# GpSimd adds the kept outer sum to C22 in SBUF and narrows each group's last row tile, with the orders of groups, beginning and end replaced

## The chip, the core and the metric

One core of one Trainium2 chip runs the kernel. TensorE (PE) multiplies matrices into PSUM, which has eight banks of 128 x 512 fp32 numbers, called b0 to b7 below. VectorE (DVE), ScalarE (ACT) and GpSimd (POOL) work on tiles of 128 partitions. SyncE (SP) issues all data transfers of this kernel, in one queue. Each engine works through its own instructions in order and waits on semaphores for the others. The metric is the time of one execution in microseconds (us).

## The reference

```python
def reference(x, w):
    cs = np.cumsum(x, axis=1)
    diff = cs - np.concatenate([np.zeros(...), cs[:, :-1, :]], axis=1)
    return np.matmul(diff, w).astype(np.float32)
```

The difference of a running sum is `x` again, so the kernel computes `x @ w`: x is 8 x 2048 x 2048, which is 16384 rows in 128 row tiles of 128, and w is 2048 x 2048, all fp32.

## The kernel before

**Beginning.** While `w` is loaded, the first four row tiles are multiplied in bf16 in the plain way (lines 347 and 394). VectorE and ScalarE then make scaled fp16 blocks of `w` (B11, B12, B21, B22 and the differences T1 to T4), and a first group of four row tiles is done by `group_plain`.

**Groups.** The other 120 row tiles are done in 30 groups of four, `group(g)`, in which the row tiles g and h = g + 2 give the upper halves A11, A12 and g + 1 and h + 1 the lower halves A21, A22. The outer scheme is Strassen's in Winograd's form with seven products: five of them, called P1 to P5, are split once more into seven inner products (`Quarters`), and S2 T2 and S3 T3 are done directly. One inner product, `slot(i)`, is four 128x512 matmuls (line 624); a piece of a direct product is four too (line 602). All banks are in use all the time. In `Quarters`, bank h[0] gathers one inner product after another; ScalarE copies it away in between: `first` copies the first product into g[0], on which slot 3 then accumulates, and `out2` and `out4` copy h[0] into SBUF, after which slots 4 and 6 write h[0] again. `middle` and `last` (line 590) are VectorE's sums of a bank and such a copy. `s1` to `s4`, the sums S1 to S4 and the sums `in1` to `in5` of weights are VectorE's sums of two fp16 operands in SBUF, line 590 too.

**Ends of the outer sums.** Bank pair X holds, late in a group, a sum that both C22 and C21 need. ScalarE keeps it, scaled, in SBUF as the beginning of C21 (`keep`, line 145), and VectorE adds it, scaled, to C22 out of the bank (`add_one`, line 649: bank times a factor plus C22). The same is done for Y, of the tiles h. When a result is whole, SP puts it to HBM (line 657, 669 for the last group).

**The next group's rows.** Each row tile is loaded in two halves (`load`, line 159), weighed by ScalarE (`weigh`, line 167: a sum of absolute values; `mean`, line 188), given a scale by VectorE (`scale`, a reciprocal, line 190), narrowed to fp16 with that scale by ScalarE (`narrow`, two halves of 128x1024, line 145) and turned by two DMA transposes (`turn`, line 218). Labels carry the tile's role: 4 and 6 are the next group's g and h, 5 and 7 its g + 1 and h + 1. So `narrow7.0` and `narrow7.1` narrow the last row tile of the next group. They run early in that group; S1h is the first sum that reads the tile, P5.s1 reads S1h, and the second product of P5 reads P5.s1.

**What sets the order.** The code only records operations, each with a label and an engine. A table of numbers, `places`, gives each label a place for the periods 0 (beginning), 1, 2, 29, 30, 31 and one common row (`None`) for all other groups; `emit` sorts all operations by it, and the engines' queues stand in that order.

Of the kernel before, what the change touches and what calls it, by code (L numbers as in the profile page):

```python
# [10 lines left out]
def kernel(  # L11
# [6 lines left out]
    nc = tc.nc  # L18
# [130 lines left out]
    def role(t):  # L149
        return t - PLAIN - 4 * period[0]  # L150
# [49 lines left out]
    def narrow_one(t, i):  # L200
        to, data, s = narrowed(t)[:, ds(i * NH, NH)], where[t][i], scales[t]
        record(f"narrow{role(t)}.{i}", "act", on_two(to, data, s))
        if i == 1 and t != PLAIN + 1:
            stage.append(where[t][1])
# [442 lines left out]
    def add_one(label, c, p, u):  # L647
        record(
            label, "dve", lambda: nc.vector.scalar_tensor_tensor(c, p, u, c, MUL, ADD)  # L649
        )  # L650

# [312 lines left out]
    def group(g):  # L964
# [206 lines left out]
        add("C22g+X", C22g, X, vg, [1])  # L1171
        keep("keep C21g", X, vg, C21g, [1])
        add("C22g+X", C22g, X, vg, [0])
# [23 lines left out]
        add("C22h+Y", C22h, Y, vh, [0])  # L1197
        keep("keep C21h", Y, vh, C21h, [1])
        add("C22h+Y", C22h, Y, vh, [1])
# [21 lines left out]
    for g in range(PLAIN + 4, END, 4):  # L1221
# [201 lines left out]
        },  # L1423
# [211 lines left out]
```

## Time and profile before

| what | before |
|---|---|
| median of 3 runs | 1448.48 us (1448.45 to 1448.72) |
| span of the profiled execution | 1446.9 us |
| granted TensorE clock | 0.999 |
| PE, DVE, ACT, POOL busy | 1439.8, 1339.8, 1193.8, 0.9 us |
| bytes moved by DMA | 351.59 MB, mean 243 GB/s |

The span is one execution as the hardware profiler saw it; the runs are timed from outside. Rows of groups read: line, engine, operation, output from input, shapes, count, busy time and mean duration of one, then the idle time of the engine just before and what ended it. Matmuls are pipelined: each has a duration of 379 ns, while the next one starts 0.216 us after it. Times on the time line and of the stretches are microseconds from the beginning of the span.

### The profile page before, as it was taken

How to read it: one execution, taken by the hardware profiler on the slowest of the kernel's cores; microseconds unless marked ns; L12 is line 12 of the kernel's file. 1: busy time of each engine (PE TensorE's matmuls, PEld its weight loads, DVE VectorE, ACT ScalarE, POOL GpSimd, SP SyncE). 2: the span in 40 equal slices, each digit the busy share in tenths (PEclk: the TensorE clock that was granted, in tenths of full speed). 3: DMA queues.
4: the chain of work that ended last, by engine and by line, in shares of the span. 5: the costliest groups of instructions: out<-in, count | busy, mean ns of one | idle time of the engine just before them, and what ended most of it. 6: DMA issues, size and time to landing. Idle time of an engine off the chain costs nothing.

```text
span 1446.9 us, 20369 instructions
## 1 busy us (share of the span) xinstructions
PE 1439.8 (100%) x6698; PEld 652.8 (45%) x6698; DVE 1339.8 (93%) x2355; ACT 1193.8 (83%) x1985; POOL 0.9 (0%) x5
## 2 busy tenths in 40 slices
PE   9999999999999999999999999999999999999998
PEld 4444444444444444444444444444444444444443
DVE  7999999999999999999999999999999999999988
ACT  4897878898888888888988888988888888889783
POOL 0000000000000000000000000000000000000000
PEclk9999999999999999999999999999999999999999
DMA  9999988899888999988898989998989998899963
GB/s 362 375 266 265 250 227 222 230 249 264 231 229 223 243 256 241 242 227 229 245 263 219 245 220 242 245 264 217 236 231 242 265 236 237 216 235 249 275 190 116
DMA packets 343930, 351.59 MB, mean 243 GB/s; under 512 B 270992, under 2 KB 270992, under 8 KB 343824
## 3 DMA queue, kind: packets, MB, share of 16 engines
q1 hardware_dynamic: 343824, 350.29, 89.4%
q8 instruction: 52, 0.85, 0.2%
q14 instruction: 54, 0.44, 0.1%
HBM read 150.99 MB, written 134.22 MB: 197 GB/s over the span
## 4 chain that ended last, share of the span: by engine, by line
PE 93%; issue 4%; DVE 1%; ACT 1%; DMA 0%; POOLq 0%; DVEq 0%
PE b L624 61%; PE b L602 32%; DVE W L146 1%; DMA out_dram<-arena 0%; ACT arena L145 0%; DVE arena L649 0%; ACT waste L167 0%; ACT F L145 0%; ACT arena L141 0%; PE b L490 0%; POOLq L1630 0%; DVE b L590 0%; DVEq L1630 0%; ACT b L141 0%; ACT tiny L194 0%
## 5 line engine op out<-in xcount | busy, mean ns | idle before, releaser
L602 PE MATMUL b<-W,x 128*128 128x512 f16 x2144 | 518.3, 379 | 0.0
L649 DVE SCALAR_TENSOR_TENSOR arena<-b,tiny,arena 128x512 f32<-128x512 f32 x612 | 448.0, 747 | 15.0 <-ACT arena L141 4.5
L624 PEld LDWEIGHTS <-arena 128*128 128x128 f16 x2744 | 268.3, 98 | 324.5 <-DVE arena L590 5.4
L624 PE MATMUL b<-W,arena 128*128 128x512 f16 x1672 | 413.8, 379 | 0.0
L145 ACT ACTIVATE arena<-b,tiny 128x512 f32<-128x512 f32 x495 | 316.3, 684 | 31.9 <-PE b L602 13.7
L602 PEld LDWEIGHTS <-x 128*128 128x128 f16 x2144 | 209.7, 98 | 253.1 <-DVE x L590 0.2
L167 ACT ACTIVATE waste<-F,tiny 128x1024 uint8<-128x1024 f32 x246 | 284.0, 1154 | 16.2 <-DMA F<-in_x_dram 14.7
L145 ACT ACTIVATE F<-F,tiny 128x1024 f16<-128x1024 f32 x245 | 280.9, 1147 | 11.7 <-DVE tiny L190 10.6
L624 PE MATMUL b<-W,x 128*128 128x512 f16 x1192 | 288.1, 379 | 0.0
L624 PE MATMUL b<-arena 128*128 128x512 f16 x1072 | 261.6, 379 | 0.1
L624 PEld LDWEIGHTS <-x 128*128 128x128 f16 x1428 | 139.7, 98 | 168.5
L590 DVE TENSOR_TENSOR b<-b,arena 128x512 f32<-128x512 f32 x298 | 206.4, 693 | 5.4 <-ACT arena L141 1.9
L141 ACT COPY arena<-b 128x512 f32<-128x512 f32 (+1 forms) x316 | 181.6, 586 | 27.1 <-PE b L624 16.2
L141 ACT COPY b<-b 128x512 f32<-128x512 f32 x149 | 85.6, 574 | 136.6 <-PE b L624 113.3
L590 DVE TENSOR_TENSOR arena<-W 128x2048 f16<-128x2048 f16 (+1 forms) x158 | 186.0, 1177 | 0.2 <-PE b L624 0.2
L590 DVE TENSOR_TENSOR arena<-x,x 128x512 f16<-128x512 f16 (+1 forms) x181 | 91.9, 508 | 50.5 <-PE b L624 50.4
L590 DVE TENSOR_TENSOR x<-x,x 128x1024 f16<-128x1024 f16 x124 | 85.4, 689 | 1.9
L590 DVE TENSOR_TENSOR arena<-W,arena 128x512 f16<-128x512 f16 (+1 forms) x157 | 86.3, 566 | 0.2 <-PE b L624 0.2
L590 DVE TENSOR_TENSOR arena<-arena 128x512 f16<-128x512 f16 x120 | 50.9, 425 | 13.7 <-PE b L624 11.8
L624 PE MATMUL b<-arena,x 128*128 128x512 f16 x236 | 60.4, 379 | 0.0
L347 PE MATMUL b<-arena 128*128 128x512 bf16 x240 | 53.8, 379 | 0.6 <-DVE arena L142 0.4
L590 DVE TENSOR_TENSOR arena<-x,arena 128x512 f16<-128x512 f16 x119 | 49.9, 419 | 0.3 <-PE b L624 0.3
(51 smaller groups left out, 494.8 us busy)
## 6 DMA issues: line engine op xcount, KB each, us to landing
F<-in_x_dram SPq DMA_DIRECT2D x246, 512.0 KB, 5.5
out_dram<-arena SPq DMA_DIRECT2D x240, 512.0 KB, 4.8
W<-in_w_dram SPq DMA_DIRECT2D x31, 512.0 KB, 9.0
out_dram<-arena SPq DMA_DIRECT2D x31, 256.0 KB, 2.7
W<-in_x_dram SPq DMA_DIRECT2D x16, 256.0 KB, 7.2
x<-F SPq DMA_TRANSPOSE x246, 4.3
arena<-in_x_dram SPq DMA_DIRECT2D x2, 512.0 KB, 5.0
W<-in_w_dram SPq DMA_DIRECT2D x2, 256.0 KB, 9.3
```

Of the source, the lines that this page charges most:

```text
L141: "act": lambda: nc.scalar.copy(to, src),
L145: "act": lambda: nc.scalar.activation(to, src, COPY, scale=scale),
L146: "dve": lambda: nc.vector.tensor_scalar(to, src, scale, None, MUL),
L167: lambda: nc.scalar.activation(waste, data, ABS, bias=least, scale=1.0 / ROW, accum_out=m),
L347: said = nc.tensor.matmul(to[n], xP[:, r, ko, :], b[:, ds(n * NB, NB)], start=(ko == 0), stop=(ko == KO - 1),)
L590: record(label, "dve", lambda: nc.vector.tensor_tensor(dst, p, q, op))
L602: said = nc.tensor.matmul(to[n], a[k], b[k][:, n, :], start=(start and k == 0), stop=(k == KH - 1), skip_group_check=True,)
L624: said = nc.tensor.matmul(to, a[k], b[k], start=(start and k == 0), stop=(k == 3), skip_group_check=True)
L649: label, "dve", lambda: nc.vector.scalar_tensor_tensor(c, p, u, c, MUL, ADD)
```

## The change

Three things change. First, the four adds of X and Y to C22 in each group of the loop read the kept copy in SBUF, not the bank, and are done by GpSimd (`sum_kept`). Second, in every period but the first, GpSimd narrows the row tile of role 7. Third, the rows 1, 2, 29, 30, 31 and `None` of `places` are replaced; row 0 stays as it was.

```diff
     def narrow_one(t, i):
         to, data, s = narrowed(t)[:, ds(i * NH, NH)], where[t][i], scales[t]
-        record(f"narrow{role(t)}.{i}", "act", on_two(to, data, s))
+        if role(t) == 7 and period[0]:
+            record(
+                f"narrow{role(t)}.{i}",
+                "pool",
+                lambda: nc.gpsimd.tensor_scalar(to, data, s, None, MUL),
+            )
+        else:
+            record(f"narrow{role(t)}.{i}", "act", on_two(to, data, s))
...
+    def sum_kept(label, c, k, halves=range(2)):
+        for n in halves:
+            sum_kept_one(f"{label}.{n}", c[:, n, :], k[:, n, :])
+
+    def sum_kept_one(label, c, k):
+        record(label, "pool", lambda: nc.gpsimd.tensor_tensor(c, c, k, ADD))
...
-        add("C22g+X", C22g, X, vg, [1])
+        sum_kept("C22g+X", C22g, C21g, [0])
         keep("keep C21g", X, vg, C21g, [1])
-        add("C22g+X", C22g, X, vg, [0])
+        sum_kept("C22g+X", C22g, C21g, [1])
...
-        add("C22h+Y", C22h, Y, vh, [0])
+        sum_kept("C22h+Y", C22h, C21h, [0])
         keep("keep C21h", Y, vh, C21h, [1])
-        add("C22h+Y", C22h, Y, vh, [1])
+        sum_kept("C22h+Y", C22h, C21h, [1])
...
         None: {
-            'C21h+P4.h.0': 937, 'P1.0': 943, 'P2.0': 977, 'P1.1': 981, 'P1.first': 1012,
+            'P4.last': 782.515, 'P1.0': 943, 'C21h+P4.h.0': 971.428, 'P1.1': 974.765,
```

The numbers tell little by themselves; what the queues hold does. Three places follow, in which line numbers after the change are 7 to 14 higher.

**PE in the second group of the loop**, at P2's first product (into b6, with x01 as weights). P2's slot 3, into b4 with the same x01, accumulates on ScalarE's copy of b6. After the change:

```order
L631 MATMUL b6_80<-W_58,x01_63 128x512
L631 LDWEIGHTS x01_63
L631 MATMUL b6_80<-W_58,x01_63 128x512
L631 LDWEIGHTS x01_63
L631 MATMUL b6_80<-W_58,x01_63 128x512
L631 LDWEIGHTS x01_63
L631 MATMUL b4_78<-W_58,x01_63 128x512
L631 LDWEIGHTS x01_63
```

Before:

```order
L624 MATMUL b6_80<-W_58,x01_63 128x512
L624 LDWEIGHTS x01_63
L624 MATMUL b6_80<-W_58,x01_63 128x512
L624 LDWEIGHTS x01_63
L624 MATMUL b6_80<-W_58,x01_63 128x512
L624 LDWEIGHTS arena_70
L624 MATMUL b0_74<-arena_70 128x512
L624 LDWEIGHTS arena_70
```

Before, four times five other matmuls stood between the last one into b6 and the first one into b4; now none does.

**VectorE in a group of the common row**, just after the group's first products, around the reciprocal that `narrow7` needs. After the change:

```order
L597 TENSOR_TENSOR arena<-W,arena 128x512 x2
L597 TENSOR_TENSOR arena<-x_66,x_67 128x1024
L597 TENSOR_TENSOR arena<-W,arena 128x512
L597 TENSOR_TENSOR x_66<-x_62,x_66 128x1024
L597 TENSOR_TENSOR arena<-x_62,x_64 128x512
L656 SCALAR_TENSOR_TENSOR arena<-b_79,tiny,arena 128x512
L597 TENSOR_TENSOR arena<-W,arena 128x512
L597 TENSOR_TENSOR arena<-x_62,arena 128x512
L597 TENSOR_TENSOR arena<-x_63,x_65 128x512
L190 RECIPROCAL tiny<-tiny 128x1
```

Before:

```order
L590 TENSOR_TENSOR arena<-W,arena 128x512 x2
L190 RECIPROCAL tiny<-tiny 128x1
L590 TENSOR_TENSOR arena<-x_62,x_64 128x512
L590 TENSOR_TENSOR arena<-W,arena 128x512
L590 TENSOR_TENSOR b_75<-b_77,arena 128x512
L590 TENSOR_TENSOR arena<-W,arena 128x512
L590 TENSOR_TENSOR arena<-x_66,x_67 128x1024
```

The rows from W are the four parts of the weight sum in1.Q4, the rows 128x1024 are S1g and S3g. Before, the reciprocal stood behind two parts of in1.Q4; now it stands behind all four, S1g, S3g, three of the inner sums and a bank's add.

**SP late in a group of the common row**, from the first half of the load of role 7 on (`F<-in_x_dram` is a load, `out_dram<-arena` a put). After the change:

```order
L159 DMA F<-in_x_dram 128x1024
L225 DMA_TRANSPOSE x_67<-F 128x8x128
L225 DMA_TRANSPOSE x_66<-F 128x8x128
L671 DMA out_dram<-arena 128x1024
L159 DMA F<-in_x_dram 128x1024
L671 DMA out_dram<-arena 128x1024
```

Before:

```order
L159 DMA F<-in_x_dram 128x1024
L218 DMA_TRANSPOSE x_66<-F 128x8x128
L159 DMA F<-in_x_dram 128x1024
L218 DMA_TRANSPOSE x_67<-F 128x8x128
L657 DMA out_dram<-arena 128x1024 x2
```

The second half of that load, `load7.1`, stood ahead of both puts of the tile g + 1; now it stands behind the first of them, put1.1, which puts the C22 that GpSimd has added to.

More of the change, by code (lines that the diff above doesn't have):

```diff
@@ L1370 @@
         1: {
[52 rows of a table removed]
-        },
[48 rows of a table removed]
[64 rows of a table added]
+        },
[56 rows of a table added]
         },
         29: {
[43 rows of a table removed]
[52 rows of a table added]
         },
         30: {
[34 rows of a table removed]
[41 rows of a table added]
         },
         31: {
-            'P4.last': 457, 'C21h+P4.h.1': 459, 'put-1.0.1': 469, 'C21h+P4.h.0': 594,
-            'put-1.0.0': 1067,
+            'P4.last': 457.284, 'C21h+P4.h.1': 457.287, 'put-1.0.1': 457.291,
+            'C21h+P4.h.0': 461.468, 'put-1.0.0': 464.683,
         },
         None: {
[43 rows of a table removed]
[53 rows of a table added]
         },
```

482 rows, old and new, of the table places are left out of this document.

## The prediction, made before the changed kernel ran

> **What bounds the kernel now.** I read the head of the page first, then the chain and the waits, then stretches of the span, and single places on the time line last.
>
> ```profile
> span 1446.9 us, 20369 instructions
> PE 1439.8 (100%) x6698; PEld 652.8 (45%) x6698; DVE 1339.8 (93%) x2355; ACT 1193.8 (83%) x1985; POOL 0.9 (0%) x5
> ```
>
> TensorE is busy throughout and GpSimd is empty. A busy PE need not run at its own pace, so I look at the chain that ended last and at everything PE and its weight loads waited for (total, times, longest):
>
> ```profile
> 251.78 12.09 PE b L624 x56
> 295.81 12.09 PE b L624 x56
> ```
>
> ```profile
> PE b L380 <- DVE arena L260: 1.2, 1, 1.2
> PE b L347 <- DVE arena L142: 0.4, 1, 0.4
> PE b L347 <- ACT arena L141: 0.2, 1, 0.2
> PEld L624 <- DVE arena L590: 5.4, 27, 0.3
> ```
>
> The same piece of the chain comes back after 44.03 us, and 12.09 us for 56 matmuls is 0.2159 us each. A group issues 51 runs of four matmuls (a quarter, below: 0.863 us); 204 x 0.2158 = 44.03. So a group is nothing but matmuls at their own pace. The three waits of PE belong to the warm-up and the plain first rows. The fourth row is a warning: about once in a group a weight load waits for a VectorE sum, and the matmul in flight just hides it.
>
> Stretches of the span (after the length: busy time of PE, PEld, DVE, ACT, POOL; then clock, DMA share, GB/s):
>
> ```profile
> 100.00:140.00 40.00, 40.00 (x187) 18.13 (x186) 39.86 (x94) 29.45 (x49) 0.00 (x0) 1.00 0.94 264
> 140.00:180.00 40.00, 40.00 (x187) 18.12 (x186) 39.86 (x78) 33.76 (x58) 0.00 (x0) 1.00 0.95 255
> 600.00:644.03 44.03, 44.03 (x206) 19.95 (x205) 40.77 (x74) 37.48 (x64) 0.00 (x0) 1.00 0.90 239
> 1400.00:1420.00 20.00, 20.00 (x95) 9.05 (x93) 18.97 (x36) 12.16 (x22) 0.00 (x0) 1.00 0.54 165
> ```
>
> PE has no gap in any of them, at clock 1.00. VectorE has 3.3 us to spare in a steady group (44.03 - 40.77), nothing from 100 to 180 us, and 5% near the end. Hence **taking work off VectorE and ScalarE shortens nothing by itself**: no matmul goes away, and PE waits for neither. A gain can only lie behind the last matmul; a loss can arise wherever a result comes later than before.
>
> **The change part by part.** In each of 30 groups four VectorE adds go, in 29 of them two ScalarE narrowings; 120 adds and 58 narrowings come on GpSimd. The rows of the work that goes:
>
> ```profile
> L649 DVE SCALAR_TENSOR_TENSOR arena<-b,tiny,arena 128x512 f32<-128x512 f32 x612 | 448.0, 747 | 15.0 <-ACT arena L141 4.5
> L145 ACT ACTIVATE F<-F,tiny 128x1024 f16<-128x1024 f32 x245 | 280.9, 1147 | 11.7 <-DVE tiny L190 10.6
> 1440.65 2.73 DVE L649 SCALAR_TENSOR_TENSOR arena<-b,tiny,arena 128x512 f32<-128x512 f32 x4
> ```
>
> (a) *Freed time.* Four adds in a row take 2.7 us of VectorE, two narrowings 2.3 us of ScalarE. PE covers both, so they are worth **0**; VectorE's room in a steady group grows from 3.3 to 6.0 us.
>
> (b) *Price on GpSimd.* No row shows such work there. I bound it by the engine that did it (0.75 and 1.15 us) and by twice that (1.5 and 2.3), and take the middle, 1.1 and 1.7: 4 x 1.1 + 2 x 1.7 = 7.8 us a group, between 5.3 and 10.6. The Trainium skill, GPSIMD Engine Reference, section "3.1 Elementwise — side-by-side cycle accounting", gives 4497 ns for a two-input fp32 add of 2048 elements, by which I estimate 1.1 us for 512; its section "4.1 Engine selection" puts one-input work at roughly line rate. If narrowing went as fast as that add (1.1), the start term in (d) would be 1.5 and the whole sum 0.8 us smaller; no run here shows it yet.
>
> (c) *A new order of products.* The first place in the section on the change shows PE going straight from P2's first product in b6 to the product that accumulates on its copy in b4. What that copy takes stands on the time line of before, at the same product:
>
> ```profile
> 165.24 1.03 PE L624 MATMUL b<-W,x 128*128 128x512 f16 x4
> 166.10 1.03 PE L624 MATMUL b<-arena 128*128 128x512 f16 x4
> 166.35 0.57 ACT L141 COPY b<-b 128x512 f32<-128x512 f32 x1
> ```
>
> The copy ends at 166.92, so b4's product could start at about 166.97, where now another starts at 166.10: **0.9** lost, which nothing hides. In the same way I counted, in the built order, the places where a bank is copied by ScalarE and written again with a single quarter between: nine in the last two groups (before: none), and two in each of 26 steady groups (before: none). From the start of the last matmul one quarter gives 0.22 + 0.86 = 1.08 us; the matmul's 0.38, the copy's 0.57 and two hand-overs of some 0.05 need 1.05. In hand are 0.03 us, and a longer ScalarE row in the way (1.15) would cost up to 1.1. I take 0.1 us a place for nine at the end and three at the start, **1.2** (0 to 2.4), and 0.1 for each steady group, **2.6** (from 0).
>
> (d) *GpSimd beside VectorE.* Line 590 holds VectorE's sums; all but those into banks read two operands from SBUF:
>
> ```profile
> 140.00:180.00 40.00, 28.34 (x55) 1.00 0.95 255
> 600.00:644.03 44.03, 27.72 (x50) 1.00 0.90 239
> L590 DVE TENSOR_TENSOR b<-b,arena 128x512 f32<-128x512 f32 x298 | 206.4, 693 | 5.4 <-ACT arena L141 1.9
> ```
>
> Less ten bank rows (6.9 us), two-operand rows fill 20.8 of 44.03 us, 47%; from 140 to 180 us, less some four, 64%. Whether they and GpSimd hold each other up no row here shows. If not, it costs 0. If each us of GpSimd stops VectorE, it costs 10.6 - 2.7 = 7.9 us once, in the loop's first group, where VectorE has no room. I take the share of two-operand rows: 0.64 x 7.8 - 2.7 = **2.3**, and **1.0** (0 to 4) for the last two groups, whose room is a third of a steady one's. In a steady group 0.47 x 7.8 = 3.7 us fit into the 6.0 of room. The rule that speaks most against the change is the Trainium skill's, SBUF — State Buffer, section "Who interferes with whom": a VectorE instruction with two SBUF inputs and a GpSimd instruction that reads SBUF exclude each other for the whole instruction. It is the third rival.
>
> (e) *New waits, and the path of the narrowed tile.* VectorE's add of P4 to C21 must now wait until GpSimd has read C21; behind it stand P2.s1, P2.s2 and the next group's sums, for which P2's and P1's products wait. The put of C22 waits for GpSimd, and behind it, by the third place shown, stands load7.1. That load begins the tightest path: load, weigh, mean, reciprocal, narrow, transpose, S1h, P5.s1, second product of P5.
>
> ```profile
> 741.35 2.33 ACT L145 ACTIVATE F<-F,tiny 128x1024 f16<-128x1024 f32 x2
> 751.43 0.67 DVE L590 TENSOR_TENSOR arena<-x,x 128x1024 f16<-128x1024 f16 x1
> 752.35 2.75 PE L624 MATMUL b<-W,arena 128*128 128x512 f16 x12
> 1436.99 0.42 DVE L590 TENSOR_TENSOR arena<-x,x 128x512 f16<-128x512 f16 x1
> 1437.33 0.69 DVE L590 TENSOR_TENSOR b<-b,arena 128x512 f32<-128x512 f32 x1
> DMA to landing us min/median/max: 3.0/4.3/7.4
> ```
>
> Before, narrowing ends at 743.7 and P5's second product starts at 752.35 + 8 x 0.216 = 754.1: 10.4 us for transposes and sums. After, with the group's first matmul at 0: the weight sum in1.Q4 waits for P1's second product, done at 0.86 + 1.03 = 1.9. By the second place shown, it and the rows up to the reciprocal follow: seven of 128x512 (0.34 from start to start), two of 128x1024 (0.6) and one add (0.7), 4.3 us in all, so narrowing starts near 6.4. In the new order P5's second product is the twentieth quarter, at 19 x 0.863 = 16.4. S1h, P5.s1 and the weight load take 0.7 + 0.4 + 0.2. There remain 8.7 us for two narrowings and a transpose's landing: 2 x 1.7 + 4.3 = 7.7 fits with 1.0 in hand, 2 x 1.15 + 3.0 with 3.4, and 2 x 2.3 + 7.4 is 3.3 late. I take **0**.
>
> **Sum**: 0.9 + 1.2 + 2.6 + 2.3 + 1.0 = 8.0 us on the span of 1446.9, 1454.9. The shown runs' median, 1448.5, lies 1.6 above that span, so **1456.5**; with each term at half or at one and a half, 1452.5 to 1460.5.
>
> **Rivals.** *Not slower* (0.20): GpSimd takes 0.75 and 1.15 us and disturbs nobody, and only the 0.9 of (c) is lost: 1449.4. For it speak 6.0 us of room; against it margins of 0.03.
>
> *Late in every group* (0.20): the wait for the narrowed tile takes the place of VectorE's load. It decides from a narrowing of 2.2 us with a landing of 4.3; at 2.3 us it is 0.2 late, with a landing of 5.1 then 1.0. Between them 0.6 x 28 groups = 17 us on top of the sum: 1473.
>
> *Full exclusion* (0.16): every us of GpSimd stops VectorE where there is no room, 7.9 at the start and 4 at the end in place of 2.3 and 1.0: 1465. It is what the page SBUF — State Buffer of the Trainium skill would make of (d).
>
> *Faster* (0.02): only the tail could give it.
>
> ```profile
> 1440.83 1.03 PE L624 MATMUL b<-W,x 128*128 128x512 f16 x4
> out_dram<-arena SPq DMA_DIRECT2D x31, 256.0 KB, 2.7
> ```
>
> Behind the last matmul's end at 1441.9 lie 5.0 us of which an add (0.7) and a put's landing (2.7) must stay; 1.6 us at most can go, less than 0.2% (2.9 us, about what a measurement of this kernel tells from no change).
>
> **Chances.** The forecast has 0.42. Slower by over 0.2%: 0.42 + 0.20 + 0.16 = 0.78; within: 0.20; faster: 0.02. The range, 1448.6 to 1482, leaves out the best part of the first rival and the worst of the second.
>
> **What would show it.** (a) is right if VectorE is busy some 38 us in a group. (c) is right if PE waits 0.9 us once near 165 us behind a ScalarE copy, and 0.05 to 0.3 at some other copies. (d) is right if two-operand rows start late or grow while GpSimd works, most of all from 150 to 200 us. (e) is wrong if P5's weights come late in every group. The whole is wrong if groups still repeat at 44.03 us from the first to the last (first rival), or at 44.4 and more (second).

## The result, and the profile after

| what | before | after |
|---|---|---|
| median | 1448.47 us (1448.22 to 1448.72) | 1480.13 us (1478.03 to 1481.12) |
| span of the profiled execution | 1446.9 us | 1477.2 us |
| VectorE, ScalarE, GpSimd busy | 1339.8, 1193.8, 0.9 us | 1289.2, 1134.4, 348.3 us |

The changed kernel is slower: the ratio is 1.0217, with a 95% interval of 1.0202 to 1.0231. The direction was forecast, the size was not: 31.7 us were lost in place of 8. One of the four runs of narrow_load10, an experiment below, took 2563.27 us at a granted clock of 0.556; its time below is the median of the other three.

The page of the changed kernel first: its head, then two groups of costly instructions (busy time and mean of one in ns, then the idle time ahead of them):

```profile
span 1477.2 us, 20562 instructions
PE 1450.1 (98%) x6692; PEld 650.9 (44%) x6698; DVE 1289.2 (87%) x2235; ACT 1134.4 (77%) x1927; POOL 348.3 (24%) x183
...
L664 POOL TENSOR_TENSOR arena<-arena 128x512 f32<-128x512 f32 x120 | 179.0, 1508 | 940.9 <-DMA out_dram<-arena 628.3
...
L206 POOL TENSOR_SCALAR F<-F,tiny 128x1024 f16<-128x1024 f32 x58 | 168.4, 2904 | 123.0 <-DVE tiny L190 120.3
```

GpSimd is 348 us busy, where 7.8 us a group had been reckoned, some 234 in all. A narrowing takes 2.9 us, 2.5 times ScalarE's 1.15. What PE itself waited for, against three short waits of the warm-up before:

```profile
PE b L631 <- ACT arena L141: 7.3, 16, 1.0
PE b L631 <- DVE arena L597: 5.2, 11, 1.4
PE b L631 <- ACT arena L145: 2.3, 2, 2.0
PE b L631 <- ACT b L141: 1.9, 3, 0.8
```

ScalarE's copies into SBUF (line 141 into arena: the `out2` and `out4`) and VectorE's sums of weights are late. These idle times are short of the loss: a matmul lasts 0.38 us, but the next one is due 0.22 us after its start, so the first 0.16 us of a late start do not show as idle time. So below, a wait is counted from the start of one matmul to the start of the next, less 0.216, each put down to its inner product. Counted so, the changed kernel loses 3.2 us in the periods 1 and 2, 19.6 in the 26 groups of the common row and 6.6 in the last two; the kernel before 0.5 in all. Behind the last matmul lie 6.1 us in place of 5.0. That makes 30.0 of the 30.3 us between the spans.

Of the 19.6 us, 13.9 stand at one place, **P1.4, the slot 4 of P1, which waits in 25 groups**; 2.8 stand at P5.1, the place that the prediction had watched. Two steady stretches (length, busy time of PE, PEld, DVE, ACT, POOL, then clock):

```profile
600.00:644.60 44.60, 44.25 (x206) 19.87 (x204) 38.97 (x70) 34.88 (x62) 11.79 (x6) 1.00 0.89 235
644.60:689.30 44.70, 44.17 (x206) 19.91 (x205) 38.98 (x68) 35.71 (x63) 11.79 (x6) 1.00 0.89 234
```

A group takes some 44.7 us for the same 44.03 us of matmuls, at clock 1.00. VectorE is only 39 us busy: freeing it was real, and worth nothing.

How P1.4 comes to wait is read backwards on the time line, here in one group: first the instructions of GpSimd's line (shortest, median and longest, ns), then the time line of VectorE, SyncE's queue, ScalarE and PE.

```profile
L664 POOL TENSOR_TENSOR arena<-arena x3: 1267/1268/2317, 520.1 to 523.7; 128x512 f32<-128x512 f32 x3
```

```profile
521.44 1.22 DVE L597 TENSOR_TENSOR arena<-W,arena 128x2048 f16<-128x2048 f16 x1
...
523.81 0.34 SPq L671 DMA_DIRECT2D out_dram<-arena  x1
524.19 0.42 SPq L159 DMA_DIRECT2D F<-in_x_dram  x1
...
529.86 1.15 ACT L167 ACTIVATE waste<-F,tiny 128x1024 uint8<-128x1024 f32 x1 [1.31 <-DMA F<-in_x_dram]
...
531.34 0.56 ACT L141 COPY arena<-b 128x512 f32<-128x512 f32 x1
...
531.96 1.02 PE L631 MATMUL b<-W,arena 128*128 128x512 f16 x4 [0.56 <-ACT arena L141]
```

The second of the three adds, C22g+X.1, is the long one: 2.3 us, because VectorE sums four parts of a weight (in1.Q1, 1.22 us) at the same time. `put1.1` waits for this add; `load7.1`, which the change placed behind that put, goes at 524.19 and has landed only at 529.86. ScalarE has nothing to do but stands in `weigh7.1` for 1.31 us; the copy P1.out2 is queued behind it, and PE waits for the copy.

Two of the forecast losses are there too: P2.3 behind ScalarE's copy of P2's first product, and VectorE's last adds behind GpSimd's last one.

```profile
171.99 1.02 PE L631 MATMUL b<-W,x 128*128 128x512 f16 x4 [0.76 <-ACT b L141]
...
1470.45 1.27 POOL L664 TENSOR_TENSOR arena<-arena 128x512 f32<-128x512 f32 x1 [2.90 <-ACT arena L145]
...
1471.75 1.41 DVE L656 SCALAR_TENSOR_TENSOR arena<-b,tiny,arena 128x512 f32<-128x512 f32 x2 [0.38 <-POOL arena L664]
```

The first is 0.92 us from start to start, against 0.9 forecast. The second belongs to the 1.0 us more behind the last matmul: part (e) of the prediction names such a wait, but gives it no time. In adds_half, below, where GpSimd adds half the columns, 0.2 us of it is left.

### The profile page after: what moved, and what is told of

It is laid out like the page before. It is cut to its first block, busy times and chain, and to the rows that moved or that the text cites. A ratio compares the mean times of both kernels' runs of the same rounds, so it can differ in the third digit from the quotient of the medians.

```text
span 1477.2 us, 20562 instructions
## 1 busy us (share of the span) xinstructions
PE 1450.1 (98%) x6692; PEld 650.9 (44%) x6698; DVE 1289.2 (87%) x2235; ACT 1134.4 (77%) x1927; POOL 348.3 (24%) x183
## 5 line engine op out<-in xcount | busy, mean ns | idle before, releaser
L609 PE MATMUL b<-W,x 128*128 128x512 f16 x2144 | 515.6, 379 | 0.0
L145 ACT ACTIVATE arena<-b,tiny 128x512 f32<-128x512 f32 x495 | 330.5, 685 | 132.5 <-PE b L609 98.9
L656 DVE SCALAR_TENSOR_TENSOR arena<-b,tiny,arena 128x512 f32<-128x512 f32 x492 | 356.1, 745 | 78.6 <-POOL arena L664 31.1
L664 POOL TENSOR_TENSOR arena<-arena 128x512 f32<-128x512 f32 x120 | 179.0, 1508 | 940.9 <-DMA out_dram<-arena 628.3
L631 PE MATMUL b<-W,x 128*128 128x512 f16 x1192 | 301.0, 379 | 2.9 <-ACT arena L145 2.0
L631 PE MATMUL b<-arena 128*128 128x512 f16 x1072 | 267.1, 380 | 1.6 <-ACT b L141 1.2
L145 ACT ACTIVATE F<-F,tiny 128x1024 f16<-128x1024 f32 x187 | 214.7, 1148 | 24.3 <-DVE tiny L190 23.2
L206 POOL TENSOR_SCALAR F<-F,tiny 128x1024 f16<-128x1024 f32 x58 | 168.4, 2904 | 123.0 <-DVE tiny L190 120.3
L597 DVE TENSOR_TENSOR arena<-W,arena 128x512 f16<-128x512 f16 (+1 forms) x157 | 104.8, 683 | 0.0
L597 DVE TENSOR_TENSOR arena<-arena,x 128x512 f16<-128x512 f16 x119 | 50.7, 426 | 4.8 <-DVE arena L597 0.5
```

The source lines that it names most:

```text
L145: "act": lambda: nc.scalar.activation(to, src, COPY, scale=scale),
L206: lambda: nc.gpsimd.tensor_scalar(to, data, s, None, MUL),
L597: record(label, "dve", lambda: nc.vector.tensor_tensor(dst, p, q, op))
L609: said = nc.tensor.matmul(to[n], a[k], b[k][:, n, :], start=(start and k == 0), stop=(k == KH - 1), skip_group_check=True,)
L631: said = nc.tensor.matmul(to, a[k], b[k], start=(start and k == 0), stop=(k == 3), skip_group_check=True)
L664: record(label, "pool", lambda: nc.gpsimd.tensor_tensor(c, c, k, ADD))
```

## The experiments

All times stand beside runs of the kernel before on the same chip, 1448.4 to 1448.7 us. First four kernels that undo or do one part.

**load71_early.** In the common row, `load7.1` goes back ahead of the transposes of role 5:

```diff
-            'load7.1': 2488.37
+            'load7.1': 2360.0
```

> One number of the changed kernel is altered: in the row of the common groups load7.1 goes ahead of both transposes of role 5 and of put1.1 in SyncE's queue. Theory 'queue' (load7.1 lands late because of its new place; ScalarE stands in weigh7.1 until it has landed, and the copy P1.out2, for which TensorE's P1.4 waits, stands behind it): the wait at P1.4, 0.56 us in each of 25 groups, goes, and most of the 2.1 us at P5.1 too, so 1480.1 - 13.9 to - 16 = 1464 to 1467. Theory 'GpSimd' (its rows are too slow, 1.27 and 2.85 us, and whatever comes earlier ahead of them is lost behind them): the wait moves from P1.4 to P5.1, about 0.6 us a group, so 1476 to 1481.

Measured: 1474.95 us (ratio 1.0181, 1.0166 to 1.0196). Neither theory had it whole. Not one wait at P1.4 is left in the common row, as "queue" said, but 11.6 us now stand at P5.1, in all 26 groups, as "GpSimd" said:

```profile
PE b L631 <- DVE arena L597: 8.9, 28, 1.0
```

How P5.1 comes to wait stands on the time line of one group: GpSimd's two narrowings, SyncE's two transposes (the second one is issued at 538.40, when the narrowings end), VectorE's S1h, and PE.

```profile
532.50 5.87 POOL L206 TENSOR_SCALAR F<-F,tiny 128x1024 f16<-128x1024 f32 x2 [4.33 <-DVE tiny L190]
...
535.46 4.17 SPq L225 DMA_TRANSPOSE x<-F  x2
...
541.54 0.69 DVE L597 TENSOR_TENSOR arena<-x,x 128x1024 f16<-128x1024 f16 x1 [1.00 <-DMA x<-F]
...
542.75 1.47 PE L631 MATMUL b<-W,arena 128*128 128x512 f16 x6 [0.25 <-DVE arena L597]
```

VectorE stands 1.00 us for the transposed tile, P5.s1 follows on S1h, and PE waits for P5.s1. So two paths of nearly equal lateness lay beside each other; mending one uncovered the other.

**adds_half.** GpSimd adds half the columns:

```diff
-        record(label, "pool", lambda: nc.gpsimd.tensor_tensor(c, c, k, ADD))
+        record(label, "pool", lambda: nc.gpsimd.tensor_tensor(
+            c[:, : NB // 2], c[:, : NB // 2], k[:, : NB // 2], ADD))
```

> The changed kernel, but GpSimd adds only the first 256 of each 512 columns, so that half of the kept sum is missing from C22; all queues stay as they are. Theory 'queue': SyncE is still in the transposes of role 5 when the add of C22g ends (522.7 against 520.9 us at the tenth group), so load7.1 goes no earlier and P1.4 waits as before: 1474 to 1480, a gain of some us at most in the last two groups and at the start. Theory 'GpSimd': the adds' 1.27 us are on the path of each group, and the loss of 0.7 us a group shrinks by half or more: below 1471.

Measured: 1468.05 us (1.0129, 1.0112 to 1.0146). "GpSimd" had named such a time (below 1471), "queue" had not. P1.4 falls from 13.9 to 10.1 us, the last two groups from 6.6 to 3.3. So the adds are on that path. "Queue" had put the end of the add at 520.9, ahead of the end of SyncE's transposes; but `put1.1` waits for the second add of C22g, which ends at 523.7.

**orders_alone.** The changed orders, the engines of before:

```diff
-        if role(t) == 7 and period[0]:
+        if False:
...
-        record(label, "pool", lambda: nc.gpsimd.tensor_tensor(c, c, k, ADD))
+        record(label, "dve", lambda: nc.vector.tensor_tensor(c, c, k, ADD))
```

> The changed kernel's orders with the work back on its old engines: VectorE adds (both operands from SBUF), ScalarE narrows role 7. Theory 'queue': load7.1 stands where it stands in the changed kernel, P1.4 waits 0.4 to 0.8 us in every group, VectorE and ScalarE are fuller than the order allows for: 1474 to 1490. Theory 'GpSimd': with nothing on GpSimd the loss goes, up to the 0.9 us at P2's first copy and some tenths: 1450 to 1457.

Measured: 1476.10 us (1.0185, 1.0170 to 1.0200), a number that "queue" had named, but for another reason: P1.4 waits in one group only. ScalarE, with 2.3 us more in each group than its order allows for, brings P5.out2 late (7.9 us at P5.4), and P5.1 loses 5.3. The orders are made for these engines; alone they tell nothing of what GpSimd costs.

**engines_steady.** The opposite: the orders of before, and in the 26 common groups the engines of the change:

```diff
+        if role(t) == 7 and 3 <= period[0] <= 28:
+            record(..., "pool", lambda: nc.gpsimd.tensor_scalar(to, data, s, None, MUL))
...
-            'C22g+X.1': 2458, ... 'C22g+X.0': 2532,
+            'C22g+X.1': 2519, ... 'C22g+X.0': 2518,
```

> The kernel before, with all its orders, but in the 26 groups of the common row GpSimd does the four adds and narrows role 7 (two numbers are altered, so that an add comes after the copy it reads). Theory 'queue': without the new place of load7.1 groups repeat at 44.03 to 44.15 us: 1448 to 1452. Theory 'GpSimd': narrowing takes 2 x 2.85 in place of 2 x 1.15 us, and the exclusion with VectorE's sums adds to it; the weights of P5 come late, 0.5 us or more in each group: 1461 and more.

Measured: 1467.99 us (1.0134, 1.0119 to 1.0150). So GpSimd's work costs 0.75 us a group in the old orders as well, a time that "GpSimd" had named, but at another place than it had named: 14.8 of the 19.6 us stand at P3.2 and P3.4, only 4.7 at P5. The next two split it.

**adds_steady** and **narrow_steady** are engines_steady with only the adds, or only the narrowing, on GpSimd.

> The kernel before with its orders, but in the 26 common groups GpSimd does the four adds (as in engines_steady, with narrowing back on ScalarE). If narrowing on GpSimd made engines_steady's 0.75 us a group: 1448.3 to 1452. If the adds, their exclusion with VectorE or their wait ahead of the puts made it: 1461 and more.

> The kernel before with its orders, but in the 26 common groups GpSimd narrows role 7, and the adds stay on VectorE. If narrowing (5.8 in place of 2.3 us ahead of turn7.1, with the loads that stand behind it in SyncE's queue) made engines_steady's 0.75 us a group: 1464 to 1470. If the adds made it: 1448.3 to 1452.

Measured: the adds alone 1449.41 us (1.0005, 0.9995 to 1.0014), the narrowing alone 1468.87 us (1.0138, 1.0123 to 1.0153). **In the old orders the narrowing makes all of it, the adds nothing.** Of the adds alone, GpSimd's group and all that PE waited for:

```profile
L653 POOL TENSOR_TENSOR arena<-arena 128x512 f32<-128x512 f32 x104 | 159.2, 1563 | 1135.6 <-ACT arena L145 1097.7 <-DMA out_dram<-arena 37.9
```

```profile
PE b L380 <- DVE arena L260: 1.2, 1, 1.2
PE b L347 <- DVE arena L142: 0.7, 2, 0.3
PE b L347 <- ACT arena L141: 0.2, 1, 0.2
```

The adds are even stretched by VectorE (1.56 us in the mean), and no group waits: here load7.1 goes ahead of the puts that wait for the adds, and the loads behind those puts go up to 0.8 us later, which nothing waits for. Of the narrowing alone, the narrowings, SyncE behind them, ScalarE and PE:

```profile
L206 POOL TENSOR_SCALAR F<-F,tiny 128x1024 f16<-128x1024 f32 x52 | 157.4, 3027 | 1165.8 <-DVE tiny L190 1163.4
```

```profile
534.86 0.87 SPq L664 DMA_DIRECT2D out_dram<-arena  x2
...
542.00 0.69 ACT L145 ACTIVATE arena<-b,tiny 128x512 f32<-128x512 f32 x1 [0.60 <-DMA out_dram<-arena]
...
549.00 0.59 ACT L141 COPY b<-b 128x512 f32<-128x512 f32 x1
...
549.64 1.02 PE L631 MATMUL b<-W,arena 128*128 128x512 f16 x4
```

Narrowing ends 3.6 us later than on ScalarE. `turn7.1` waits for it at the head of SyncE's queue; load10.0 and the put of C21h (the first of the two at 534.86) stand behind. ScalarE needs that put's buffer and stands 0.60 us; its queue is late by 1.1 us from there on, and P3.first (549.00) and P3.out2 come late for P3.2 and P3.4, 13.5 us in all.

**narrow_load10** is narrow_steady with one more number, by which that load passes the transpose:

```diff
-            'load10.0': 3075
+            'load10.0': 3020
```

> As narrow_steady, and in SyncE's queue load10.0 goes ahead of turn7.1 (both wait for the end of narrow7.1; load10.0 so goes 1.24 us earlier, turn7.1 0.6 later, and P5's second product has 1.7 us in hand behind turn7.1). Theory 'queue behind the transpose' (narrowing ends 3.6 us later than before, turn7.1 waits for it in SyncE's queue, load10.0 lands late, ScalarE stands in weigh6.0 and the copies P3.first and P3.out2 behind it come late for P3.2 and P3.4, 13.5 us in 25 groups): these waits go, 0.2 us a group at P5.2 and P5.3 stays: 1454 to 1459. Rival 'exclusion' (the narrowing holds up VectorE's sums, and that shift goes on to P3): nothing changes, 1466 to 1470.

Measured: 1486.94 us (1.0258, 1.0237 to 1.0278), above both forecasts. The waits at P3.2 and P3.4 went, but 30.7 us appeared at P5.2, which waits for VectorE's sums:

```profile
PE b L631 <- DVE arena L597: 26.8, 26, 3.2
```

With the load ahead of it, the transpose lands 4.9 us after its issue; and P5.2 comes ahead of P5.1 in this order, so the 1.7 us in hand, which I had read at P5.1, were not there. The test does not show what a load passed ahead is worth.

**load71_scale7.** load71_early, and the reciprocal goes earlier, so that narrowing can begin 1.0 us sooner:

```diff
-            'scale7': 2797.466
+            'scale7': 2742.0
```

> As load71_early, and the reciprocal that the narrowing of role 7 needs goes ahead of in1.Q4.2, P1.s4 and P2.s3 in VectorE's queue, so that GpSimd may narrow 1.3 us earlier, but beside three or four VectorE rows that read two operands from SBUF. Theory 'two paths' without a price of exclusion: P5.1 comes in time, 1460 to 1464. Rival 'exclusion': the rows of 0.42 us and the narrowing hold each other up, a narrowing takes 3.5 us or more or VectorE's rows 1 us, the gain is eaten: 1468 to 1478.

Measured: 1473.36 us (1.0171, 1.0154 to 1.0188), as "exclusion" had it. VectorE's rows at the time, the first one the reciprocal, and the narrowings (shortest, median, longest):

```profile
531.30 0.15 DVE L190 RECIPROCAL tiny<-tiny 128x1 f32<-128x1 f32 x1
531.37 0.40 DVE L597 TENSOR_TENSOR arena<-W,arena 128x512 f16<-128x512 f16 x1
531.69 0.42 DVE L597 TENSOR_TENSOR arena<-x,arena 128x512 f16<-128x512 f16 x1
532.02 0.41 DVE L597 TENSOR_TENSOR arena<-x,x 128x512 f16<-128x512 f16 x1
532.36 0.42 DVE L597 TENSOR_TENSOR arena<-x,arena 128x512 f16<-128x512 f16 x1
```

```profile
L206 POOL TENSOR_SCALAR F<-F,tiny x58: 2842/2888/3947, 167.6 to 1429.5; 128x1024 f16<-128x1024 f32 x58
```

The narrowing starts at 531.55, behind the reciprocal, and takes 3.95 us in place of 2.9, beside VectorE's four sums, which keep their 0.4 us each. It ends where it ended without the edit (9.5 us behind the group's first matmul in both), and P5.1 waits nearly as before, 10.7 us in all for 11.6.

**load71_half_narrow.** load71_early, and VectorE narrows the second half:

```diff
+        if role(t) == 7 and i == 1 and 3 <= period[0] <= 28:
+            record(f"narrow{role(t)}.{i}", "dve", on_two(to, data, s))
...
-            'narrow7.1': 2900.701
+            'narrow7.1': 2830.0
```

> As load71_early, and in the 26 groups of the common row VectorE narrows the second half of role 7 (one row of about 0.75 us, in a gap that its queue has behind P1.middle), while GpSimd narrows the first half alone. Theory 'two paths' (the changed kernel loses a steady group's 0.7 us on two paths that run beside each other, so that mending one uncovers the other: GpSimd's add, stretched from 1.27 to 2.3 us by the exclusion with VectorE's sum, then put1.1, load7.1, weigh7.1 on ScalarE, the copy P1.out2, P1.4; and GpSimd's two narrowings of 2.9 us, turn7.1, S1h, P5.s1, P5.1): both waits go, groups repeat at 44.03 to 44.2 us, 1475 - 0.45 x 26 = 1460 to 1464; about 12 us of start and end stay. Rival 'exclusion everywhere' (what counts is that GpSimd's rows hold up VectorE's sums wherever they meet): half a narrowing less changes little, 1470 to 1475.

Measured: 1502.44 us (1.0370, 1.0354 to 1.0385), a miss by a fault of the experiment. The second half is narrowed into the memory that the first half is read from, so it can't start before the first is done; VectorE stood ahead of it until 9.5 us of the group, and P2.5 waited 31.6 us in all behind. It tells nothing about the two theories.

**half_on_scalar** repairs that: load71_scale7, and the first half is narrowed by ScalarE, in a gap of its queue, the second by GpSimd:

```diff
+        if role(t) == 7 and i == 0 and 3 <= period[0] <= 28:
+            record(f"narrow{role(t)}.{i}", "act", on_two(to, data, s))
...
-            'narrow7.0': 2812.662
+            'narrow7.0': 2780.0
```

> The changed kernel with three edits in the 26 common groups: load7.1 ahead of role 5's transposes (as in load71_early), role 7's reciprocal ahead of in1.Q4.2 (as in load71_scale7), and narrow7.0 on ScalarE, in the gap that its queue has behind unit4; GpSimd narrows the second half alone, 2.9 us in place of 5.8, and all its adds stay. Theory 'two paths': narrowing ends near 9.6 us of the group in place of 12.4, P5.1 and P1.4 wait no more, groups repeat at 44.03 to 44.2, and only the losses of the start, the end and the tail stay (12 us): 1458 to 1464. Rival (the new orders lose 0.4 to 0.7 us a group by their own margins, whoever narrows): 1468 to 1476.

Measured: **1456.88 us** (1.0056, 1.0039 to 1.0073), a little below the range of "two paths" and far from the rival's. Two steady stretches again:

```profile
600.00:644.03 44.03, 44.03 (x206) 19.96 (x205) 38.96 (x69) 36.21 (x62) 8.85 (x5) 1.00 0.89 238
644.03:688.06 44.03, 44.03 (x206) 19.95 (x205) 38.96 (x69) 36.20 (x62) 8.85 (x5) 1.00 0.91 239
```

With one narrowing in place of two on GpSimd, and all four adds and the new order of products still there, the groups repeat at 44.03 us and PE has no gap. So the lateness of the load and of the narrowing, not the orders' own margins, made the loss of the steady groups. From load71_scale7 to here, 16.5 us went with this one move. The common row loses 1.8 us, 1.4 of it in its first group; the first two periods 3.1, the last two 3.2, the tail 1.0.

**start_new** and **end_new** put the changed rows of the beginning, or of the end, into the kernel before. Where rows of the two tables meet, some operations stand in another order than they were recorded in, so part of the sums is of the wrong data; the amount of work is the same.

> The kernel before, with the changed kernel's orders and engines in the periods 1 and 2 alone. The changed kernel lost 3.2 us there: 0.9 at P2.3 (the copy with nothing between), 0.95 at P1.2 (ScalarE in weigh7.1, which waits for load7.1), 0.6 at P3.0 and P3.1, 0.4 in the period ahead. If these are made by these rows themselves: 1451 to 1453. If they come from the groups behind (the common row): below 1450.

> The kernel before, with the changed kernel's orders and engines in the last two groups and the end alone; the narrowing for the last group but one stays on ScalarE. The changed kernel lost 6.6 us ahead of its last matmul there and 1.5 behind it. If the late narrowing of the common row makes the first part (P1.4, P5.2, P3.0 and P5.4 of the last group but one wait for load7.1, turn7.1 and load10.0): about 1.5 for the GpSimd add in the tail and 0.6 for P2.2, 1450 to 1452. If the end's own orders make it: 1454 to 1457.

Measured: 1458.98 us (1.0070, 1.0054 to 1.0085) and 1454.79 us (1.0043, 1.0028 to 1.0057). In start_new the periods 1 and 2 lose 4.0 us, with 0.92 at P2.3 again, but 6.2 more are lost in the group behind, where the tables meet. In end_new the last two groups lose 5.4 and the tail 1.0; the largest wait, 1.9 at P1.4, is that of a narrowing on ScalarE where the new row has no room for it. The time of end_new is one that "the end's own orders" had named; that of start_new lies above both of its forecasts. Both fit the beginning's and the end's own rows better than the other reading, but the seams spoil them; they settle no more than P2.3 and the tail.

## Why the prediction was wrong

The step that failed is (e): it put the new waits and the path of the narrowed tile at 0, and they made most of the 19.6 us of the common row (13.9 at P1.4, 2.8 at P5.1; 1.8 us of the row are left in half_on_scalar, where both paths come in time). It failed in two ways, by a price that (b) had too low and by a path that was not followed to its end.

- **What bounds the kernel, and (a): right.** PE at its own pace is the floor; VectorE's work fell to 39 us a group ("some 38") and nothing came of it. adds_steady shows it by itself: 1.0005.
- **(b) had the narrowing too cheap.** The price of a narrowing was bounded by ScalarE's row (1.15) and twice that (2.3), and 1.7 was taken; it is 2.89 us in the median. Twice a neighbour's row was no bound, only a guess. The add was inside its bounds: 1.27 us in the median, 1.1 taken. The figure that the Trainium skill gives for an add (GPSIMD Engine Reference, section "3.1 Elementwise — side-by-side cycle accounting"; an estimate of 1.1 us by it) was near; the rule of section "4.1 Engine selection", that one-input work runs roughly at line rate, is not what the trace shows: 2.9 us for 1024 columns, 2.5 times ScalarE.
- **(e) followed the right path and got the wrong sum.** At 2.89 us, the 8.7 us that it had left are overdrawn: two narrowings and its landing of 4.3 come to 10.1. Narrowing starts 6.6 us behind the group's first matmul and ends at 12.4, S1h starts 3.2 us after that, at 15.6, and P5.1 waits 0.45 us a group once load71_early bares it. This was the second rival (0.20, "late in every group", from a narrowing of 2.2 us): right in its place, and its 1473 was nearest of all cases.
- **(e) missed the other path.** The load behind the put was named, but only followed towards P5.1. What counted first was what is queued behind the waiting instruction on ScalarE: `weigh7.1` waits for the load, and P1.out2 stands behind it. 13.9 us.
- **(c) was right at one place and wrong as a rule.** P2.3 lost 0.92 us (0.9 forecast). The margins of 0.03 us at tight copies, priced at 2.6 us in the steady groups, cost nothing: half_on_scalar has the same order of products and no gap.
- **(d) had the mechanism of the third rival and the wrong size.** The exclusion is there, row by row, in both directions. In the steady groups of half_on_scalar it costs nothing, though all four adds are there; what it cost in the first and the last groups was not separated. It shows where a row that others wait for stands in it: the narrowing of load71_scale7 (3.95 us for 2.9), which ate what the earlier reciprocal had won, and the add ahead of `put1.1` (2.3 for 1.27). How much of the 13.9 us that stretch alone makes no run shows.
- **Start and end**, 5.4 us of the sum, measured 12 in the changed kernel (3.2, 1.3 in the common row's first group, 6.6, 1.0) and 8.7 in half_on_scalar, so about 3 of them came from the late loads and narrowings of the common row too. Which part of the rest is made by which row was not settled.

No version beats the kernel before. adds_steady is level with it, within what can be measured; VectorE is busy for 1299.5 us there in place of 1339.8, and TensorE has no use for it.

## What to carry to other kernels

Work moved to an idle engine is not free if its result is waited for: price the path, not the load, and if no row shows the operation on that engine, ask what happens at three times its neighbour's duration. Follow a late transfer to the engine that will stand waiting for it, and read what is queued behind that instruction; it may be late long before the tile itself is missed. When a fix uncovers an equal wait elsewhere, two paths were late together, and only mending both tells what either cost.

## What the hardware showed that I had not expected

The exclusion between VectorE and GpSimd can be read in durations. A VectorE sum with both operands in SBUF that meets a GpSimd add waits within its own row (time line of the changed kernel):

```profile
205.15 1.46 DVE L597 TENSOR_TENSOR arena<-x,arena 128x512 f16<-128x512 f16 x1
```

```profile
L664 POOL TENSOR_TENSOR arena<-arena x1: 1272/1272/1272, 205.1 to 205.1; 128x512 f32<-128x512 f32 x1
```

The second fence is the add that it meets (line view, one instruction). The sum takes 1.46 us in place of 0.42 and ends some 0.3 us behind the add. This agrees with the Trainium skill's SBUF — State Buffer, section "Who interferes with whom", by which a VectorE instruction with two SBUF inputs and a GpSimd instruction that reads SBUF exclude each other. Sums of a bank and a copy are not stretched: line 597 from banks has a mean of 694 ns beside 693 before. But a narrowing excludes VectorE for only a part of its time. In narrow_steady one of two starts at 530.0 and takes 2.84 us, the shortest; below them VectorE's time line:

```profile
L206 POOL TENSOR_SCALAR F<-F,tiny x2: 2844/3018/3192, 526.8 to 530.0; 128x1024 f16<-128x1024 f32 x2
```

```profile
530.55 0.87 DVE L597 TENSOR_TENSOR arena<-x,arena 128x512 f16<-128x512 f16 x1
531.35 0.41 DVE L597 TENSOR_TENSOR arena<-x,x 128x512 f16<-128x512 f16 x1
```

The first sum takes 0.87 us in place of 0.41, so it waits until some 1.0 us into the narrowing; the second passes freely inside it, and the narrowing is not stretched. The two sums read so in 24 of the 26 groups. Here that section's "for the whole instruction" does not hold.

A pause of TensorE can cost more than itself. In the last group but one of the changed kernel PE waited 2.2 us at P3.0, and the clock fell after it:

```profile
1400.00:1402.80 2.80, 1.80 (x7) 0.78 (x7) 1.82 (x4) 2.37 (x5) 0.00 (x0) 0.83 1.13 309
1402.80:1405.20 2.40, 2.24 (x7) 0.51 (x6) 1.74 (x4) 1.19 (x2) 0.00 (x0) 0.50 0.25 55
```

Six matmuls came 0.2 us late each, 1.2 us in all. About half of this is a loss of its own: in load71_early, at clock 1.00, P5.4 waits 1.2 us there, of which 0.6 is left here, where the matmuls ahead of it are late. In narrow_load10 pauses of 2.9 and 3.4 us at P5.2 were each followed by clock 0.50, with 8 and 14 late matmuls behind them. But after its pause of 2.5 us at P3.0 load71_early shows clock 1.00, so a pause of this length does not always do it.
